# Transposing the normalised rows of a hybrid layer's first pass on TensorE through two PSUM banks, where DMA transposed them

## The chip, the cores and the metric

The kernel runs on one core of a Trainium2 chip. The metric is device time in microseconds (us) of one execution. TensorE (PE in the rows; its weight loads are PEld), VectorE (DVE), ScalarE (ACT), GpSimd (POOL) and SyncE (SP) each work off a queue of their own in order; an instruction that waits holds up all that stand behind it on its engine. In this kernel every transfer is issued from SP's queue.

## The reference

One decoder layer over 4096 rows of width 1024 (float32). What matters here is its beginning:

```
h    = rms_norm(x) * norm_gain
proj = h @ w_in            # 3328 columns: gMLP u, v, gate; attention q, k, v, gate; memory q, gate
kv   = rms_norm(mem) * mem_gain @ w_mem_kv      # 256 memory tokens
...                        # gMLP gating, dilated attention (8 heads), attention into the memory
out  = x + concat(branches) @ w_out
```

## The kernel before

Rows are worked in 32 tiles of 128. A matrix product needs its left operand transposed (the 1024 columns on partitions), and nearly full precision is had by splitting each number into a high and a low float16 part and adding three products. So `proj` issues, for each of 8 slices of 128 columns, three matmuls of 512 columns: 24 for a result of 512 columns.

The program has a first pass (pass A), two more passes over the rows (B and C, with the attention of the 8 heads interleaved) and a last loop for the output. Pass A does, for each tile n:

- `rows(n)`, three tiles ahead of the products: load x (tile name `x_a`), then `norm_rows`: ScalarE squares and sums (`xj_a`, L236), VectorE and GpSimd make the scale (`xs_a`, L237 and L238), ScalarE writes the high part and VectorE the low part of `xh_a` (L240, L241; two buffers), and the pair is transposed into `xTa` (L242; four buffers). `xTa` is also stored in device memory for passes B and C (`xTd`, L339).
- `pv`: 24 matmuls (L222) of `xTa` with the value weights, taken out of PSUM by ScalarE and VectorE into `vt` (L274, L276).
- `pq`: 24 matmuls with the query and key weights of four heads, taken out by ScalarE into `rw_q` (L248), squared (`sq_q`, L250), reduced on VectorE (L252, L258), raised to the power -1/2 on GpSimd (`r_q`, L260), scaled on VectorE (L267, L269), split into `hl` (ScalarE L287, VectorE L288), transposed by a DMA into `stgA` (L290), put in another order by GpSimd (`stpA`, L291) and stored.

`pv` and `pq` share two PSUM banks (tag `pj`). The maxima that scale the weights pass through small PSUM tiles (`pt_wV`, `pt_wQ`, `pt_wM`, L157 and L162, read last on VectorE at L179). `ps_tile` puts tag `tr` onto tag `po`, which has two banks; in pass A only these weight tiles use it. The 256 memory tokens go through `norm_rows` too (`xh_m`, into `mTs`).

The order on each engine is made by a scheduler from a model of the program when the kernel is built, so an edit of one helper can move instructions all through the program. The line that the edit replaces is the last of `norm_rows`:

```
        Q.dma_start_transpose(dst.rearrange("p a k t -> p (a k) t"),
                              hl.rearrange("p a k -> p (a k)"))
```

Of the kernel before, what the change touches and what calls it, by code (L numbers as in the profile page):

```python
# [9 lines left out]
F16 = mybir.dt.float16  # L10
# [8 lines left out]
P = 128  # L19
# [3 lines left out]
KT = D // P  # L23
# [48 lines left out]
def tile_hybrid_layer(ctx, tc, x, mem, norm_gain, w_in, gv_gain, wsT, gb, aqg, akg,  # L72
                      mem_gain, w_kv, mqg, mkg, w_out, out):
    nc = tc.nc
    V, S, G, TE, Q = nc.vector, nc.scalar, nc.gpsimd, nc.tensor, nc.sync
# [6 lines left out]
    def ps_tile(tag, shape, dt, name):  # L82
        return pp.tile(shape, dt, tag="po" if tag == "tr" else tag, name=name)
# [17 lines left out]
    idh = cp.tile([P, P], F16, name="idh")  # L101
# [124 lines left out]
    def load_rows(pool, src, nm):  # L226
        xt = pool.tile([P, D], F32, name=f"x_{nm}", tag="xin", bufs=4)
        Q.dma_start(xt, src)
        return xt

    def norm_rows(pool, src, dst, nm, xt=None):
        if xt is None:
            xt = load_rows(pool, src, nm)
        junk = pool.tile([P, D], BF16, name=f"xj_{nm}", tag="xj", bufs=1)
        ss = pool.tile([P, 2], F32, name=f"xs_{nm}", tag="xs", bufs=3)
        S.activation(junk, xt, AF.Square, accum_out=ss[:, 0:1])  # L236
        V.tensor_scalar(ss[:, 0:1], ss[:, 0:1], 2.0 ** -30, EPS * 2.0 ** -20, ALU.mult, ALU.add)  # L237
        G.tensor_tensor(ss[:, 1:2], ss[:, 0:1], mhalf[:, 0:1], ALU.pow)  # L238
        hl = pool.tile([P, 2, D], F16, name=f"xh_{nm}", tag="xh", bufs=2)
        S.activation(hl[:, 0, :], xt, AF.Copy, scale=ss[:, 1:2])  # L240
        V.scalar_tensor_tensor(hl[:, 1, :], xt, ss[:, 1:2], hl[:, 0, :], ALU.mult, ALU.subtract)  # L241
        Q.dma_start_transpose(dst.rearrange("p a k t -> p (a k) t"),  # L242
                              hl.rearrange("p a k -> p (a k)"))


    def head_rs(pool, ps, nh, scs, scales, nm):
# [81 lines left out]
    with tc.tile_pool(name="pA", bufs=2) as pA:  # L328
# [7 lines left out]
        def rows(n, xt=None):  # L336
            xTs[n] = sk.tile([P, 2, KT, P], F16, name=f"xTa{n}", tag="xT", bufs=4)
            norm_rows(pA, x[n * P:(n + 1) * P, :], xTs[n], f"a{n}", xt)
            Q.dma_start(xT_d[n], xTs[n].rearrange("p a k t -> p (a k t)"))  # L339
# [35 lines left out]
        for n in range(NT):  # L375
# [53 lines left out]
            if n == 10:  # L429
                for j in range(2):  # L430
                    norm_rows(pA, mem[j * P:(j + 1) * P, :], mTs[:, j], f"m{j}")
            if n == 12:
                wM, scM = got("wM")
                for j in range(2):
# [5 lines left out]
                    hl = pm.tile([P, 8, 2, HD], F16, name=f"mhl{j}", tag="hl", bufs=2)  # L440
# [481 lines left out]
    for n in range(NT):  # L922
        if n + 2 < NT:
            prep_y(n + 2)
        yT, a, xr = yTs.pop(n)
# [53 lines left out]
```

## Time and profile before

| | us |
|---|---|
| median of 3 runs | 2269.75 (2264.73 to 2272.71) |
| the profiled execution | 2285.33 |
| its span, first to last instruction | 2283.6 |
| from the start to the first `pq` matmul | 53.2 |
| from there to the first `pq` matmul of the 26th tile | 341.1 |
| from there to the end of pass A's products | about 73 |
| passes B and C and the output | about 1816 |

The profiled execution took 1.7 us more than its span and 15.6 us more than the median of the runs. A busy share is the time in which an engine had at least one instruction under way. "x" counts instructions. In a row on a wait, the engine and line ahead of the arrow waited, and what stands behind it ended the wait.

### The profile page before, as it was taken

The numbers are of one execution on the slowest core, as the hardware profiler recorded it, in microseconds if no ns is written. First come the engines' busy times: TensorE is split into PE (matmuls) and PEld (weight loads), VectorE is DVE, ScalarE is ACT, GpSimd is POOL, SyncE is SP. The second block draws the span as 40 slices with busy tenths as digits, with TensorE's granted clock in tenths as the row PEclk, the third lists the DMA queues.
The fourth block names the chain that finished last, engine by engine and source line by source line (L and its number), as shares of the span: only waits on it lengthen the run. The fifth ranks groups of instructions, "written<-read, shape, count | busy, mean of one in ns | idle before, by whom it ended". The sixth has DMA issues, their size and how long they took to land. (4 is left out here: it accounts for less than half of the span.)

```text
span 2283.6 us, 43678 instructions
## 1 busy us (share of the span) xinstructions
PE 2020.8 (88%) x15969; PEld 1248.7 (55%) x15969; DVE 1563.5 (68%) x4297; ACT 985.1 (43%) x1886; POOL 975.4 (43%) x696
## 2 busy tenths in 40 slices
PE   4888888978799899799999998998989998888888
PEld 3333333434356456465676775765756765555556
DVE  6776655477777778688786876876767576656553
ACT  6333432222246446465575674654757741101000
POOL 1455455465367568574464452553635520000000
PEclk8999999989899999799999998999999999999999
DMA  9999797765355765755646446345454379999996
GB/s 267 212 217 233 184 224 167 185 167 158 114 159 123 207 152 146 181 126 157 165 101 146 115 100 168 92 116 131 91 122 103 73 191 209 234 224 223 225 220 148
DMA packets 606232, 375.48 MB, mean 164 GB/s; under 512 B 431681, under 2 KB 541377, under 8 KB 604225
## 3 DMA queue, kind: packets, MB, share of 16 engines
q1 hardware_dynamic: 606016, 372.69, 67.9%
q8 instruction: 125, 2.05, 0.4%
q14 instruction: 91, 0.74, 0.1%
HBM read 198.52 MB, written 113.84 MB: 137 GB/s over the span
## 5 line engine op out<-in xcount | busy, mean ns | idle before, releaser
L521 POOL TENSOR_TENSOR pl<-e,ph 128x512 f16<-128x512 f32 (+1 forms) x384 | 414.6, 1094 | 310.0 <-ACT ph L520 231.4
L222 PE MATMUL pc<-wC,xTc 128*128 128x512 f16 (+1 forms) x2304 | 484.4, 354 | 8.7 <-DVE r_wO L160 7.6
L222 PE MATMUL fps<-wO,fyT 128*128 128x256 f16 (+1 forms) x2304 | 355.0, 317 | 48.7 <-DMA fyT<-fhl 48.6
L474 DVE CUSTOM_DVE_ANT_0 jk<-pa,mask 128x256 bf16<-128x256 f32 (+1 forms) x768 | 302.2, 393 | 62.8 <-PE pa L467 44.1
L571 ACT ACTIVATE e<-e,gas 128x512 f32<-128x512 f32 (+1 forms) x384 | 253.1, 673 | 181.2 <-DVE e L569 178.7
L222 PEld LDWEIGHTS <-fyT 128*128 128x128 f16 x2304 | 227.8, 100 | 175.0 <-DMA fyT<-fhl 55.6
L222 PEld LDWEIGHTS <-xTc 128*128 128x128 f16 x2304 | 225.5, 101 | 166.4 <-issue 25.0
L222 PEld LDWEIGHTS <-xTa 128*128 128x128 f16 x1608 | 164.9, 103 | 265.3 <-issue 95.9
L569 DVE TENSOR_TENSOR e<-s,mask 128x512 f32<-128x512 f32 (+1 forms) x384 | 234.0, 625 | 75.9 <-PE s L566 57.5
L222 PEld LDWEIGHTS <-xTb 128*128 128x128 f16 x1536 | 152.7, 101 | 179.2 <-issue 31.5
L222 PE MATMUL pv<-wV,xTa 128*128 128x512 f16 (+1 forms) x840 | 195.5, 396 | 52.8 <-DVE vt L276 37.0
L520 ACT CAST ph<-e 128x512 f16<-128x512 f32 (+1 forms) x384 | 211.5, 567 | 31.0 <-PE o L591 19.6
L222 PE MATMUL pqb<-wQ,xTb 128*128 128x512 f16 x768 | 196.9, 400 | 11.5 <-DMA xTb<-xTd 7.4
L291 POOL COPY stpA<-stgA 128x1024 f16<-128x1024 f16 x32 | 153.0, 4801 | 103.3 <-DMA stgA<-hl 52.3
L564 PE MATMUL s<-q,k 128*128 128x256 f16 (+1 forms) x768 | 180.9, 267 | 16.2 <-DMA q<-qkpd 7.9
L291 POOL COPY stpB<-stgB 128x1024 f16<-128x1024 f16 x32 | 153.6, 4800 | 96.4 <-DMA stgB<-hl 75.6
L222 PE MATMUL pag<-wAG,xTb 128*128 128x512 f16 x768 | 188.2, 389 | 3.9 <-DVE sg L699 3.6
L222 PE MATMUL pq<-wQ,xTa 128*128 128x512 f16 x768 | 175.7, 386 | 16.0 <-ACT rw_q L248 11.0
L467 PE MATMUL pa<-kp,qn 128*128 128x256 f16 (+1 forms) x768 | 139.3, 271 | 48.8 <-DVE mx L474 41.3
L741 ACT ACTIVATE fhl<-fy,fa 128x1024 f16<-128x1024 f32 x32 | 36.7, 1148 | 333.2 <-DMA fyT<-fhl 328.2
L566 PE MATMUL s<-q,k 65*128 65x256 f16 (+1 forms) x768 | 173.1, 268 | 3.1 <-DMA q<-cm 3.1
L587 PE MATMUL o<-vr,ph 128*128 128x65 f16 x1368 | 169.9, 194 | 3.5 <-ACT ot L596 2.4
(271 smaller groups left out, 3502.7 us busy)
## 6 DMA issues: line engine op xcount, KB each, us to landing
vr<-vd SPq DMA_DIRECT2D x48, 520.0 KB
fo<-od SPq DMA_DIRECT2D x96, 260.0 KB
od<-ot SPq DMA_DIRECT2D x128, 130.0 KB
x_a<-in_x_dram SPq DMA_DIRECT2D x32, 512.0 KB
xTd<-xTa SPq DMA_DIRECT2D x32, 512.0 KB
xTb<-xTd SPq DMA_DIRECT2D x32, 512.0 KB
xTc<-xTd SPq DMA_DIRECT2D x32, 512.0 KB
fx<-in_x_dram SPq DMA_DIRECT2D x32, 512.0 KB
```

Source lines behind the costliest of these rows:

```text
L222: TE.matmul(ps[:, :n], xt[:, a, k, :], w[:, b, k, c:c + n], start=(k == 0 and a == 0 and b == 0), stop=(k == KT - 1 and a == 1))
L291: G.tensor_copy(stp[:, :, half].rearrange("p s (r j) -> p s j r", r=R16), stg[:, :, half].rearrange("p s (j r) -> p s j r", r=R16))
L467: TE.matmul(pa[:, i, 256 - w:256], qn[:, q0:q0 + (P - 1) * d + 1:d], packed(kp, d, r, max(b - 1, 0), w), start=True, stop=True)
L474: V.tensor_tensor_reduce(jk[:, :w], pa[:, i, 256 - w:256], masks[d][:, 256 - w:256], 1.0, -3e38, ALU.add, ALU.max, mx[:, mc:mc + 1])
L520: S.copy(ph[:, :w], e[:, :w])
L521: G.tensor_sub(pl[:, :w], e[:, :w], ph[:, :w])
L564: TE.matmul(st[:, i, :n], k1[:, kk], packed(q1, d, r, b, n), start=True, stop=False)
L566: TE.matmul(st[:, i, :n], k2[:, kk], packed(q2, d, r, b, n), start=False, stop=True)
L569: V.tensor_tensor(e[:, :w], st.rearrange("p a q -> p (a q)")[:, :w], masks[d][:, :w], ALU.add)
L571: S.activation(e[:, :w], e[:, :w], AF.Exp, scale=asg[:, 2:3])
L587: TE.matmul(o[:, slot, 0:65], hi[:, c:c + 128], v[:, 0:65], start=(j == 0), stop=False)
L741: S.activation(hl[:, 0, :], y, AF.Copy, scale=a[:, 1:2])
```

## The change

`norm_rows` calls a new function `transposed`. TensorE transposes the 8 slices of the high part into one PSUM bank and the 8 slices of the low part into the other (tag `po`, float16, multiplied by a float16 identity), ScalarE copies the first bank into `xTa`, and VectorE the second. It holds for the 32 tiles of x and the two tiles of memory tokens. The other DMA transposes (of `hl`, and those of later passes) stay.

```diff
         S.activation(hl[:, 0, :], xt, AF.Copy, scale=ss[:, 1:2])
         V.scalar_tensor_tensor(hl[:, 1, :], xt, ss[:, 1:2], hl[:, 0, :], ALU.mult, ALU.subtract)
-        Q.dma_start_transpose(dst.rearrange("p a k t -> p (a k) t"),
-                              hl.rearrange("p a k -> p (a k)"))
+        transposed(dst, hl, nm)
+
+    def transposed(dst, hl, nm):
+        for a in range(2):
+            pt = ps_tile("po", [P, KT, P], F16, f"pt{nm}_{a}")
+            for k in range(KT):
+                TE.transpose(pt[:, k, :], hl[:, a, k * P:(k + 1) * P], idh)
+            if a == 0:
+                S.copy(dst[:, a], pt)
+            else:
+                V.tensor_copy(dst[:, a], pt)
```

Lines behind the edit stand 9 further down in the changed kernel (L248 becomes L257). Three places show what the scheduler made of it; numbers at the ends of names tell tiles apart.

ScalarE in the middle of pass A, one tile's worth of rows, before:

```order
L240 ACTIVATE xh_a_2412<-x_a_2405,xs_a_2408 128x1024
L274 ACTIVATE vt_2218<-pv_2193 128x8x64
L236 ACTIVATE xj_a_2707,xs_a_2708<-x_a_2705 128x1024
L287 CAST hl_15_2169<-rw_q_15_2155 128x8x64
L248 COPY rw_q_16_2250<-pq_2223 128x512
L250 ACTIVATE sq_q_16_2252<-rw_q_16_2250 128x512
```

and after:

```order
L257 COPY rw_q_14_2448<-pq_2421 128x512
L250 COPY xTa_2467<-pta_0_2478 128x1024
L259 ACTIVATE sq_q_14_2450<-rw_q_14_2448 128x512
L240 ACTIVATE xh_a_2701<-x_a_2694,xs_a_2697 128x1024
L236 ACTIVATE xj_a_3093,xs_a_3094<-x_a_3091 128x1024
L283 ACTIVATE vt_2524<-pv_2499 128x8x64
L296 CAST hl_14_2462<-rw_q_14_2448 128x8x64
```

The copy out of the first bank (`pta_0`) has come between the two instructions that take up a `pq`, and `xh_a` now follows it.

GpSimd in the middle of pass A, before:

```order
L260 TENSOR_TENSOR r_q_17_2347<-r_q_17_2347,mhalf 128x8
L291 COPY stpA_2249<-stgA_2248 128x8x8x16
L275 MEMSET vt_2563 128x8x2
L238 TENSOR_TENSOR xs_a_2887<-xs_a_2887,mhalf 128x1
L291 COPY stpA_2249<-stgA_2248 128x8x8x16
L260 TENSOR_TENSOR r_q_18_2478<-r_q_18_2478,mhalf 128x8
L275 MEMSET vt_2653 128x8x2
```

and after:

```order
L300 COPY stpA_2140<-stgA_2139 128x8x8x16
L269 TENSOR_TENSOR r_q_14_2452<-r_q_14_2452,mhalf 128x8
L238 TENSOR_TENSOR xs_a_3094<-xs_a_3094,mhalf 128x1
L284 MEMSET vt_2636 128x8x2
L300 COPY stpA_2447<-stgA_2446 128x8x8x16
L269 TENSOR_TENSOR r_q_15_2558<-r_q_15_2558,mhalf 128x8
L238 TENSOR_TENSOR xs_a_3202<-xs_a_3202,mhalf 128x1
```

Before, the power of one tile (`r_q_17`) stands ahead of the reordering copies of the two tiles before it; after, the copy of the tile before always stands ahead of a tile's power.

TensorE where a weight tile's maximum is broadcast (L162) in the middle of pass A, before:

```order
L222 LDWEIGHTS xTa_1729
L222 MATMUL pq_2130<-wQ_204,xTa_1729 128x512
L162 MATMUL pt_wQ_2493<-r_wQ_2495,ones_185 128x2
L222 LDWEIGHTS xTa_1908
L222 MATMUL pv_2193<-wV,xTa_1908 128x512
```

and after:

```order
L162 MATMUL pt_wQ_2803<-r_wQ_2805,ones_185 128x2
L222 LDWEIGHTS xTa_2467
L222 MATMUL pv_2873<-wV,xTa_2467 128x512
L248 LDWEIGHTS xh_a_2849
L248 MATMUL pta_1_2862<-idh,xh_a_2849 128x128
```

One product behind the broadcast there now stands a transpose, whose bank is the one that `pt_wQ` holds. Four weight tiles in the middle of pass A (two of `wM`, two of `wQ`) stand so.

## Rows read from the trace of the kernel before

**Rows 1.** The page: the span, and TensorE's busy time (share of the span).

```profile
span 2283.6 us, 43678 instructions
...
PE 2020.8 (88%) x15969; PEld 1248.7 (55%) x15969; DVE 1563.5 (68%) x4297; ACT 985.1 (43%) x1886; POOL 975.4 (43%) x696
```

**Rows 2.** Stretches: window, length, engines' busy us, granted clock, DMA share, GB/s.

```profile
0.00:53.00 53.00, 24.35 (x156) 18.31 (x157) 37.49 (x111) 30.77 (x64) 8.50 (x31) 0.91 0.96 265
53.00:394.00 341.00, 287.12 (x1218) 124.60 (x1218) 216.31 (x385) 132.29 (x232) 169.77 (x98) 0.92 0.93 206
394.00:467.00 73.00, 68.90 (x312) 30.62 (x310) 35.69 (x57) 19.93 (x35) 40.07 (x19) 0.98 0.74 179
467.00:2283.00 1816.00, 1640.40 (x14286) 1075.13 (x14284) 1274.05 (x3745) 802.14 (x1556) 757.06 (x550) 0.95 0.63 153
```

**Rows 3.** Waits from 53 to 394 us: us in total, times, longest.

```profile
ACT xh_a L240 <- DMA xTa<-xh_a: 79.4, 19, 8.8
...
POOL stpA L291 <- DMA stgA<-hl: 37.7, 13, 7.1
...
PE pv L222 <- DVE vt L276: 33.9, 13, 4.0
...
PE pq L222 <- ACT rw_q L248: 10.1, 4, 3.9
```

**Rows 4.** Instructions on `xTa`: ns shortest/median/longest, first and last start in us.

```profile
L222 PE MATMUL pq<-wQ,xTa x768: 376/379/634, 53.2 to 467.4; 128*128 128x512 f16 x192
L242 SPq DMA_TRANSPOSE xTa<-xh_a x32: 1806/3949/7421, 10.4 to 428.9; - x32
```

**Rows 5.** Timeline of TensorE: start, length of a run of instructions, what.

```profile
332.97 5.34 PE L222 MATMUL pv<-wV,xTa 128*128 128x512 f16 x24 [0.65 <-DVE vt L276]
...
638.48 0.45 PE L491 MATMUL pm<-idh,mv 128*32 128x128 f16 x5
```

**Rows 6.** Single lines: ns shortest/median/longest, first and last start in us.

```profile
L491 PE MATMUL pm<-idh,mv x40: 219/219/230, 638.5 to 1692.0; 128*8 128x128 f16 x32, 128*32 128x128 f16 x8
...
L596 ACT COPY ot<-o x192: 348/370/462, 666.7 to 1840.4; 128x260 f32<-128x260 f32 x192
...
L276 DVE SCALAR_TENSOR_TENSOR vt<-pv,vt x31: 401/680/693, 49.9 to 463.4; 128x512 f16<-128x512 f32 x29, 128x256 f16<-128x256 f32 x2
...
L241 DVE SCALAR_TENSOR_TENSOR xh_a<-x_a,xs_a,xh_a x32: 1272/1286/5057, 9.1 to 413.7; 128x1024 f16<-128x1024 f32 x32
```

**Rows 7.** Timeline, 436 to 450 us: one tile's way through GpSimd.

```profile
436.57 1.64 POOL L260 TENSOR_TENSOR r_q<-r_q,mhalf 128x8 f32<-128x8 f32 x1
...
439.95 0.58 ACT L248 COPY rw_q<-pq 128x512 f32<-128x512 f32 x1
440.08 0.69 DVE L288 TENSOR_TENSOR hl<-rw_q,hl 128x512 f16<-128x512 f32 x1 [0.68 <-ACT hl L287]
...
440.80 1.24 SPq L290 DMA_TRANSPOSE stgA<-hl  x1
...
443.58 4.74 POOL L291 COPY stpA<-stgA 128x1024 f16<-128x1024 f16 x1 [5.31 <-DMA stgA<-hl]
...
447.93 1.65 POOL L260 TENSOR_TENSOR r_q<-r_q,mhalf 128x8 f32<-128x8 f32 x1
```

**Rows 8.** Timeline, 0 to 75 us: the start of pass A.

```profile
17.22 6.47 PE L222 MATMUL pv<-wV,xTa 128*128 128x256 f16 x31 [4.82 <-DMA xTa<-xh_a]
...
21.71 10.28 SPq L242 DMA_TRANSPOSE xTa<-xh_a  x2
...
26.25 0.38 PE L162 MATMUL pt_wV<-r_wV,ones 1*128 1x2 f32 x2 [0.59 <-DVE r_wV L161]
...
28.13 0.15 DVE L179 TENSOR_SCALAR sc_wV<-pt_wV 128x1 f32<-128x1 f32 x1
...
31.65 6.81 PE L222 MATMUL pv<-wV,xTa 128*128 128x256 f16 x38 [5.03 <-DMA xTa<-xh_a]
```

**Rows 9.** Timeline of TensorE: the first `pq` of the first and of the 26th tile.

```profile
53.22 1.01 PE L222 MATMUL pq<-wQ,xTa 128*128 128x512 f16 x2 [1.75 <-ACT wQ L172]
...
394.27 1.03 PE L222 MATMUL pq<-wQ,xTa 128*128 128x512 f16 x4
```

## The prediction

> **What bounds the kernel now.** I read the page, then the stretches of pass A, the waits in its middle, the instructions on `xTa`, and last two pieces of timeline. The page says that TensorE is busy for 88% of a span of 2283.6 us [rows 1]: on the whole this is a TensorE kernel, and what the change is worth must be found in the stretches in which it acts. Those are pass A's: its start (0 to 53 us), its middle (53 to 394) and its last tiles (394 to 467) [rows 2]. There the DMA share is 0.96, 0.93 and 0.74, against 0.63 later.
>
> How far is the middle from TensorE's own limit? 24 matmuls of 512 columns that follow each other closely took 5.34 us [rows 5]; the last of them lasts 0.379 [rows 4], so they start (5.34 - 0.379) / 23 = 0.2157 us apart, and the 48 of a tile take 10.35. The middle holds 1218 records [rows 2]: 1218 x 0.2157 = 262.7 us of 341. About 54 us are idle (341 - 287.1 busy), and 24 us of the busy time went to half clock: the mean granted clock is 0.92, so (1 - 0.92) / 0.5 = 16% of 341 = 55 us stood at 1.2 GHz, which costs half of that, 27, much the same.
>
> What TensorE idled for is PSUM: 33.9 us on `vt` and 10.1 on `rw_q`, evictions by VectorE and ScalarE [rows 3]. ScalarE was busy for only 132 of 341 us, so it was late because it stood: it waited 79.4 us, 19 times, up to 8.8 each, in `xh_a` (L240) for the DMA transposes `xTa<-xh_a` that still read the buffer which it wanted to overwrite [rows 3]. Queued behind `xh_a` on ScalarE are just `vt`, `hl` and `rw_q`, as its order shows. So the transposes hold ScalarE, ScalarE holds PSUM, and PSUM holds TensorE.
>
> **What goes.** 34 DMA transposes. Each occupies SP's queue for 3.95 us at the median [rows 4], 134 us in all, with the x and weight loads behind it. Each moves 128 x 2048 x 2 bytes = 0.52 MB, 17.8 MB in all; at the middle's 206 GB/s with a share of 0.93, 221 GB/s when full, that is 81 us of the DMA engines. The 79.4 us of waiting on ScalarE go with them, because TensorE will have read `xh_a` long before.
>
> **What comes, on TensorE.** 34 x 16 = 544 transposes of 128 columns. The kernel has such an operation: five of them took 0.45 us [rows 5], one lasts 219 ns [rows 6], so they start (0.45 - 0.219) / 4 = 0.058 us apart. The bounds are 0.058 and 0.219; I take 0.058, for 16 stand in a row. A tile then costs 0.92 us more, all 34 cost 31.5, and a tile's floor is 11.3. The Trainium skill's page "TensorE: Matmul & The Clock Gate", Part 4: PE-mode transpose, puts one at some 275 ns in a kernel's context; by that, with none overlapping, the 544 would take 150 us and the sum below would be +94 in place of -24.5. The row agrees with such a length (219) and not with such a distance.
>
> **On ScalarE and VectorE.** ScalarE copies 1024 float16 out of PSUM: 0.58 us for 512 elements [rows 7] and 0.37 for 260 [rows 6] make 0.82 ns an element, so 1.0 us. It has the room: 132 + 27 x 1.0 = 159 us busy in the middle. For VectorE the nearest is `vt`, 512 elements from PSUM in 0.68 [rows 6]: 1.2 for 1024 (bounds 0.6, if 16-bit elements go in pairs, and 5.1, the longest `xh_a` [rows 6], if such a copy is held as that one was). `vt` never passed 0.693 in 31 times though it too reads PSUM, hence the low value. VectorE would be busy for 216 + 32 = 248 us.
>
> **The new pace of the middle.** With ScalarE free, the next loop is through GpSimd. The order after has a tile's `stpA` ahead of the next tile's `r_q`, always. Then power, scaling, `hl`, DMA transpose, `stpA`, next power make a ring. In rows 7 it ran so once, nearly undisturbed: from 436.57 to 447.93 us, 11.4, with 2.8 from the issue of the transpose to `stpA`. So at best the ring is as quick as TensorE's 11.3. `stpA` waited for its transpose 2.9 us on average where it waited, up to 7.1 [rows 3]; part of that goes with the large transposes. I take 11.9 a tile (bounds 11.4 and 13.2, today's pace: 341.05 us from the first tile to the 26th [rows 9], less 10.35 for the memory tokens' 48 matmuls, over 25 tiles).
>
> New middle: TensorE's work 262.7 + 27 tiles x 0.92 = 287.5; the ring, 0.6 x 26 = 16; four places where a transpose waits for the bank of a weight tile, from the broadcast to its last reader 28.13 + 0.15 - 26.25 = 2.0 us each [rows 8], 8 (bounds 0 and 16; what is queued behind it on TensorE is a product, so it counts in full); and half clock, a third of today's 27 since it followed the idling, 9. Together 320.5, that is 20.5 less (bounds: 296, -45, and 341, 0).
>
> **The start.** TensorE waited 4.82 + 5.03 us for `xTa` [rows 8], and two transposes held SP for 10.28 with a weight load behind them. Against that stand some five copies on VectorE (busy for 37 of 53 us): 6 us. I take -6 (bounds -12 and 0).
>
> **The last tiles and the rest.** From 394 on TensorE is near its floor; two more tiles' transposes cost 1.8: +2. The last three tiles have no rows left to transpose. Passes B and C and the output are the same instructions; the scheduler has moved them among each other, by some tens of places in the middle of the program, and I put this at 0 with 8 us either way, 0.4% of 1816, which is a judgement.
>
> Sum: -20.5 - 6 + 2 = -24.5. The profiled execution took 2285.33, 1.7 more than its span, so a profile of the changed kernel should take about 2261; on the scale of the runs, 2269.75 - 24.5 = **2245 us**.
>
> **Rivals.** (a) The ring through GpSimd takes the place of the wait: `stpA` late by 2 us in each tile leaves the pace at 13.2. The middle stays at 341, the start gives 6, the last six tiles, now at 11.7, lose 1.5 each: 9 - 6 = +3, about 2273. For it: the strict order, and `stpA`'s 37.7 us of waiting. Against: that waiting came with a DMA share of 0.93, and the ring at 432 to 450 us kept to 11.4.
>
> (b) All goes at TensorE's floor: middle 296, start -12, some 55 in all: 2214. For it: evictions were all that TensorE waited for. Against: the ring has no slack.
>
> (c) Slower, through TensorE's clock. Today 16% of the middle is at 1.2 GHz. If the transposes between the products let the clock fall more often, it costs what the waits give back: a TensorE that is slower also covers the ring's 16 us, so the gain is gone when the loss at half clock reaches 9 + 24.5 + 16 = 50 us, which is 100 us of the middle at 1.2 GHz, a mean grant of 0.85. At 0.80 it loses 68, and the time is 2269.75 + 18 = 2288. For it: a stretch with much idling does fall. Against: today's five transposes at 638 stand amid products, and without idling the last tiles got 0.98. The Trainium skill says, on the same page and in the same part, that transposes don't count as busy for the clock gate. No row here settles this.
>
> (d) Transposes that do not overlap: 544 x (0.219 - 0.058) = 88 us more on TensorE, about 2333. The row of five speaks plainly against it.
>
> **How the numbers follow.** My forecast (-10 to -45): 0.63. (b): 0.09. (a): 0.13. (c): 0.10. (d): 0.02. Passes B and C off by more than the 8 allowed, either way: 0.03. The likeliest case gives the time; 8 in 10 are held by 2218 (towards b) to 2274 (takes in a, leaves c and d out). The likeliest case alone runs from 2225 to 2260. About 0.3%, 7 us, is what a measurement of this kernel can tell from no change. Faster by more: 0.63 + 0.09 = 0.72 with the larger share of the last 0.03 set against edges of (a); within: 0.13; slower by more: 0.10 + 0.02 and the rest, 0.15.
>
> **What would show it.** In the changed kernel's profile: no wait of `xh_a` on a DMA; transposes (L248) about 58 ns apart; copies near 1.0 and 1.2 us; the first `pq` near 47 us and the 26th near 368; a DMA share of about 0.75 in the middle; and `stpA` followed at once by `r_q`. I am wrong if pass A still ends near 467 us, if the middle's granted clock is below 0.85, or if the stretch behind pass A changes length by more than 8 us.

## The result and the profile after

The changed kernel took 2291.81 us (median of 4 runs, 2285.06 to 2296.01) against 2267.24 for the kernel before in the same sitting (4 runs, 2261.01 to 2272.71): a ratio of 1.0093, 95% interval 1.0071 to 1.0116. I had forecast a gain of 24.5 us; it lost 21 to 25. The profiled execution of after took 2292.64 us, like its other runs; that of before, 2285.33, was longer than any of its timed runs, so lengths in the two profiles are compared with some 10 us of doubt for the whole program, less for a stretch.

The stretches of the changed kernel, in the columns of [rows 2]:

```profile
0.00:53.00 53.00, 29.62 (x211) 23.51 (x211) 37.93 (x113) 32.59 (x64) 8.32 (x31) 0.88 0.69 219
53.00:394.00 341.00, 306.88 (x1706) 151.81 (x1706) 215.93 (x405) 157.22 (x262) 172.03 (x98) 0.95 0.65 170
394.00:467.00 73.00, 63.80 (x311) 29.26 (x309) 25.55 (x68) 19.00 (x35) 34.53 (x20) 0.98 0.56 138
467.00:2283.00 1816.00, 1634.48 (x14269) 1074.58 (x14268) 1271.36 (x3745) 803.51 (x1559) 756.77 (x549) 0.96 0.64 153
```

What the change was to do, it did. The DMA share of the middle fell from 0.93 to 0.65, TensorE's busy time rose by 20 us, ScalarE's by 25, and the clock did not fall: 0.95 against 0.92 [rows 2]. The new operations, by line:

```profile
L248 PE MATMUL pta<-idh,xh_a x512: 218/219/314, 7.4 to 423.3; 128*128 128x128 f16 x171
...
L250 ACT COPY xTa<-pta x32: 989/1015/1019, 8.7 to 428.0; 128x1024 f16<-128x1024 f16 x32
...
L252 DVE COPY xTa<-pta x32: 677/684/692, 11.8 to 428.3; 128x1024 f16<-128x1024 f16 x32
```

The waits from 53 to 394 us, in the columns of [rows 3]:

```profile
ACT hl L296 <- DVE rw_q L278: 103.5, 21, 11.7
POOL stpA L300 <- DMA stgA<-hl: 83.1, 17, 11.8
DVE rw_q L276 <- POOL r_q L269: 60.1, 20, 10.7
...
PE pv L222 <- ACT rw_q L257: 14.6, 2, 11.5
...
PE pv L222 <- DVE vt L285: 13.0, 6, 4.5
```

The row with 79.4 us at the head of [rows 3], ScalarE's `xh_a` behind a DMA, is gone. In its place stands the ring: `stpA`'s wait for its DMA transpose went from 37.7 to 83.1 us, and `hl` and `rw_q`, which follow the power, wait 103.5 and 60.1. The first and the 26th tile's `pq` on TensorE's timeline, as in [rows 9]:

```profile
56.23 1.01 PE L222 MATMUL pq<-wQ,xTa 128*128 128x512 f16 x2 [0.42 <-ACT wQ L172]
...
386.27 1.46 PE L222 MATMUL pq<-wQ,xTa 128*128 128x512 f16 x6
```

The start is 3 us later, the middle 11 shorter (330.0 against 341.1), and from the 26th tile to the end of the last `pq` it takes 82.2 us where it took 73.5. So pass A ends at 468.5 us, before it was 467.8: nothing is left of what the missing DMA transposes gave. Of the 24.6 us between the medians some 20 or more are then lost behind it. The two profiles alone don't show that loss: in them the stretch behind pass A is 6.6 us longer (1822.4 against 1815.8), because the profiled execution of before was 15.6 us above its median.

The turn with the copy's longest wait for its transpose, around tile 16:

```profile
281.60 1.66 POOL L269 TENSOR_TENSOR r_q<-r_q,mhalf 128x8 f32<-128x8 f32 x1
...
283.11 0.43 SPq L306 DMA_DIRECT2D qkpd<-stpA  x1
283.59 1.06 SPq L351 DMA_DIRECT2D vd<-vt  x1
...
285.13 0.69 DVE L297 TENSOR_TENSOR hl<-rw_q,hl 128x512 f16<-128x512 f32 x1 [0.68 <-ACT hl L296]
...
291.21 0.33 SPq L323 DMA_DIRECT2D kp<-qkpd  x1
291.64 1.27 SPq L299 DMA_TRANSPOSE stgA<-hl  x1
...
295.67 4.71 POOL L300 COPY stpA<-stgA 128x1024 f16<-128x1024 f16 x1 [11.84 <-DMA stgA<-hl]
299.99 1.65 POOL L269 TENSOR_TENSOR r_q<-r_q,mhalf 128x8 f32<-128x8 f32 x1
```

The halves are ready at 285.8, but SP's queue stands behind `kp<-qkpd`, a load of head 0 that has to wait for a write issued at 283.1; the transpose goes out at 291.6, the copy starts at 295.7, and the next power at 300.0: 18.4 us for one turn. Some turns are longer for other reasons: 25.2 us from the power at 323.62, when VectorE was held up by a weight tile's preparation, and 21.2 from 223.9, with the memory tokens in between.

The copy does not always stand ahead of the next tile's power, as I had read from the order. In 9 of 31 turns the power ran first, 6 of them in the middle, and the copy then started right behind it, beside VectorE's scaling:

```profile
149.47 1.64 POOL L269 TENSOR_TENSOR r_q<-r_q,mhalf 128x8 f32<-128x8 f32 x1 [4.83 <-DVE m_wM L149]
...
151.82 4.75 POOL L300 COPY stpA<-stgA 128x1024 f16<-128x1024 f16 x1 [0.65 <-DMA stgA<-hl]
151.88 4.34 DVE L278 TENSOR_TENSOR rw_q<-rw_q,gaq 128x256 f32<-128x256 f32 x1
```

The scaling by `gaq` (L278) took 4.34 us here, and 0.42 without a copy beside it. The experiments come back to this.

### The profile page after: what moved, and what is told of

The parts are those of the page before. It is cut to its first block, busy times and chain, and to the rows that moved or that the text cites. A ratio compares the mean times of both kernels' runs of the same rounds, so it can differ in the third digit from the quotient of the medians.

```text
span 2290.9 us, 44788 instructions
## 1 busy us (share of the span) xinstructions
PE 2037.2 (89%) x16513; PEld 1281.0 (56%) x16513; DVE 1551.5 (68%) x4331; ACT 1012.3 (44%) x1920; POOL 971.7 (42%) x696
## 4 chain that ended last, share of the span: by engine, by line
PE 41%; DMA 14%; DVE 7%; ACT 3%; issue 3%; POOL 2%; SPq 1%; DVEq 0%; POOLq 0%; ACTq 0%
PE pc L222 12%; PE fps L222 11%; DMA fyT<-fhl 7%; PE pqb L222 3%; PE s L573 2%; PE s L575 2%; PE pag L222 2%; DMA qm<-q2t 2%; PE pa L476 2%; DVE e L578 1%; DMA cm<-rw 1%; POOL pl L530 1%; PE o L600 1%; PE o L598 1%; PE o L596 1%
## 5 line engine op out<-in xcount | busy, mean ns | idle before, releaser
L222 PE MATMUL pv<-wV,xTa 128*128 128x512 f16 (+1 forms) x840 | 183.7, 376 | 28.2 <-ACT rw_q L257 14.6
L573 PE MATMUL s<-q,k 128*128 128x256 f16 (+1 forms) x768 | 176.2, 264 | 18.2 <-DVE e L578 10.0
L598 PE MATMUL o<-vr,ph 128*128 128x64 f16 x1368 | 170.4, 194 | 0.0
```

What stands on the lines that cost most here:

```text
L222: TE.matmul(ps[:, :n], xt[:, a, k, :], w[:, b, k, c:c + n], start=(k == 0 and a == 0 and b == 0), stop=(k == KT - 1 and a == 1))
L573: TE.matmul(st[:, i, :n], k1[:, kk], packed(q1, d, r, b, n), start=True, stop=False)
L598: TE.matmul(o[:, slot, 0:64], hi[:, c:c + 128], v[:, 66:130], start=False, stop=False)
```

## The experiments

Three questions: does the ring set pass A's pace, what lost the time behind pass A, and does a saving in pass A reach the end. "Pass A alone" means that all behind pass A is left out and zeros are written. The five groups (e1 to e4, e5 to e8, and so on; e17 and e18) ran on five chips, on which the kernel before took from 2262.5 to 2286.0 us, 1% apart. Ratios of full programs are to the kernel before on the same chip. Times of pass A alone are safe within a group; e7, e8, e13 and e17 are set beside e1 across chips, which can account for some 4 us with e7 and e8 and 2 with e13 and e17. In the tables "middle" is from the first to the 26th tile's `pq`, "end" the end of the last.

**e1, e2: pass A alone, with the change and without.** The edit, in both:

```
-    at_cm = tc.tile_pool(name="at", bufs=2)
...
+    tc.strict_bb_all_engine_barrier()
+    for n in range(NT):
+        Q.dma_start(out[n * P:(n + 1) * P, :], zr)
```

> The changed kernel cut off behind pass A: passes B and C, the attention and the output loop are left out, and zeros are written to the output instead (32 writes of 512 KB behind a barrier, the same in all four kernels of this group). Theory 1 (the change gains a little in pass A, and the whole program loses it behind): the first 26 tiles came 8 us earlier in the full trace (386.3 against 394.3), so this one ends 5 to 15 us before its counterpart without the change. Rival 2 (pass A itself is no faster or is slower with the change): within 3 us of the counterpart, or behind it.

> The kernel before, cut off behind pass A in the same way (the same parts left out, zeros written). It is the counterpart of the run above: theory 1 has it 5 to 15 us longer than the changed one, rival 2 level with it or shorter.

548.17 us (544.77 to 549.7) and 552.49 (549.89 to 553.88): 4.3 us shorter with the change. Middle 337.4 and 345.5, end 472.2 and 480.1. A little was gained, between the 5 that theory 1 asked for and the 3 of rival 2; the +21 of the whole program is not in pass A.

**e3, e4: the copy `stgA` into `stpA` on ScalarE.** With the change and without, pass A alone:

```
-        G.tensor_copy(stp...
+        (S.copy if g == 0 else G.tensor_copy)(stp...
```

> The changed kernel's pass A alone (same parts left out, zeros written), with the copy stgA into stpA on ScalarE instead of GpSimd, so that the power of the next tile no longer stands behind 4.8 us of copy on GpSimd. Theory 1 (the ring power, scaling, halves, DMA transpose, copy, next power sets the pace of about 12 us a tile): the pace falls to 10.6 to 11, and the program is 20 to 35 us shorter than the changed pass A alone. Rival 2 (TensorE with its transposes and the banks of the weight preparation set the pace): within 5 us of it. Rival 3 (ScalarE now waits for the DMA transpose in its turn, and the ring closes there): longer by more than 5 us.

> The kernel before, pass A alone, with the same move of the copy to ScalarE. If the transposes of x by DMA set the pace there (13.2 us a tile), the move changes nothing: within 5 us of the counterpart without it, and the change is then worth 25 to 45 us between this run and the changed one with the move. If the ring through GpSimd sets the pace before too, it is 15 us shorter or more.

615.6 and 602.64 us: 67 and 50 longer. For e3 rival 3 held; neither expectation for e4 had it longer. The copy takes as long on ScalarE as on GpSimd, and ScalarE, which also empties PSUM, now stands for the DMA transpose in its own queue (e3):

```profile
L300 ACT COPY stpA<-stgA x32: 4713/4747/5033, 83.1 to 557.8; 128x1024 f16<-128x1024 f16 x32
...
ACT stpA L300 <- DMA stgA<-hl: 70.7, 21, 8.0
```

**e5, e6: the order behind pass A held.** The work behind pass A is the same 20,509 instructions in both programs, but the scheduler's simulated clock arrives there at another time and orders them otherwise. e5 is the changed kernel with them chained, on each engine, in the order of the kernel before; e6 the kernel before with the order of the changed one:

```
+    for i0, i1 in zip(seq, seq[1:]):
+        tc.add_manual_dep(i1, i0.name, mybir.DependencyInfo(
+            mybir.DependencyClass.NoSync, mybir.DependencyReason.DATA), reason="order")
```

> The changed kernel in full, with every instruction behind pass A (passes B and C, attention, output loop) held on its engine in the order that the scheduler gave it in the kernel before. Pass A alone was 4.3 us shorter with the change (548.17 against 552.49 us). Theory 1 (the loss behind pass A is nothing but the other order that the scheduler gave that work): 2 to 8 us shorter than the kernel before, a ratio of 0.9965 to 0.999. Rival 2 (the transposes by TensorE leave something behind that slows the rest, whatever its order): as slow as the changed kernel was, 1.007 to 1.012.

> The kernel before in full, its pass A untouched (transposes by DMA), with every instruction behind pass A held in the order that the scheduler gave it in the changed kernel. Theory 1 (the order costs the time): 20 to 32 us slower than the kernel before, a ratio of 1.009 to 1.014, without any transpose by TensorE. Rival 2 (something that the transposes leave behind): level with the kernel before, 0.998 to 1.002.

e5: 2267.12 us, ratio 1.0022 (1.0004 to 1.004), 5 us slower. e6: 2276.19, ratio 1.005 (1.0027 to 1.0072), 11 us slower without one transpose by TensorE. Theory 1 had the direction of both and was too bold in size: the order costs 11 us by e6, 16 by the step from the change to e5, and about 5 us of the change's loss are not the order. That holding an order costs nothing in itself is not shown: no run holds the kernel before in its own order and changes nothing else (e16 below, with its own order held and one further edit, stands at 0.9999). Pass A ended at 470.6 and 471.4, that is level.

**e7, e8: breaking the ring in two places.** Pass A alone. e7 queues a tile's copy on GpSimd, with the write that follows it (`flush`), behind the next tile's power; with that, e7 also issues each of head 0's loads one tile later, since they read what is written there. e8 leaves these loads out.

```
         qn = qk_split(pool, ps, 8, scs, f"q{g}_{n}", agn, 4)
+        if late:
+            with tc.issue_after(pows[-1].ins):
+                flush()
...
-            if n % 8 == 7:
-                load_max(0, (n - 7) * P, (n + 1) * P)
+            if n == NT - 1:
+                flush()
+            if n and n % 8 == 0 or n == NT - 1:
+                load_max(0, (n - 1) // 8 * 8 * P, ((n - 1) // 8 + 1) * 8 * P)
```

```
-            if n % 8 == 7:
-                load_max(0, (n - 7) * P, (n + 1) * P)
```

> The changed kernel's pass A alone (the rest left out, zeros written, as in e1), with the copy stgA into stpA of a tile queued on GpSimd behind the power of the next tile, so that no power waits for a DMA transpose through GpSimd's queue. Theory 1 (the ring through GpSimd sets the pace): the 26 middle tiles, 337 us in e1, fall to 295 to 315, and the program from 548 to 510 to 530 us. Rival 2 (TensorE, the weight preparation or ScalarE's order set it, and the ring only looks long because others wait): 543 to 550 us.

> The changed kernel's pass A alone (as in e1), without the loads of the first head's keys and queries that pass A issues on the sync engine's queue behind every eighth tile (they are left out). In the full trace the halves' DMA transpose of tile 16 was issued about 6 us after its halves, behind such a load that waited. Theory 1 (the ring stands still when its transpose is held in that queue): four loads' stalls go, 6 to 14 us shorter than 548. Rival 2 (the queue is not what holds the transposes): within 3 us.

529.07 and 530.85 us, against 548.17 in e1. e8 gained 17.3 us, some 13 of them if 4 are the chip's, where theory 1 gave it 6 to 14; 5 were in the last tiles and 8 in the middle. e7's total just fits, the reason given for it does not: its middle stayed at 336.7 us (295 to 315 expected) and only the last tiles were quicker, 10.8 us a tile against 12.5, which it may owe to the later loads (e8, without them, took 11.6). So GpSimd's queue was not all of it. VectorE by line in the middle; mean ns stand behind the busy time. From e1:

```profile
L276 DVE TENSOR_TENSOR rw_q<-rw_q,r_q 128x512 f32<-128x512 f32 x24 | 24.2, 1008 | 59.4 <-POOL r_q L269 59.3
```

From e7, where the line is L278, and then the copy and this operation on the timeline:

```profile
L278 DVE TENSOR_TENSOR rw_q<-rw_q,r_q 128x512 f32<-128x512 f32 x25 | 63.7, 2549 | 30.3 <-POOL r_q L271 30.2
...
L263 DVE TENSOR_REDUCE r_q<-sq_q 128x8 f32<-128x512 f32 x25 | 17.1, 683 | 12.8 <-ACT sq_q L261 12.7
...
L287 DVE SCALAR_TENSOR_TENSOR vt<-pv,vt 128x512 f16<-128x512 f32 x22 | 15.0, 682 | 1.4 <-ACT vt L285 1.4
```

```profile
366.96 4.76 POOL L314 COPY stpA<-stgA 128x1024 f16<-128x1024 f16 x1
367.04 4.58 DVE L278 TENSOR_TENSOR rw_q<-rw_q,r_q 128x512 f32<-128x512 f32 x1 [1.42 <-POOL r_q L271]
```

The product of `rw_q` with `r_q`, 0.69 us alone, ends within 0.1 us of the copy that began just before it. In e7 the copy stands right behind the power, where VectorE wants to scale: in 16 of the 32 tiles the scaling began during the copy and took 4.57 us at the median, in the other 16 never more than 0.69. So what GpSimd's queue no longer held, VectorE now waited out. The reduction, with one input, and `vt`, with one in PSUM, keep their lengths. The Trainium skill, "SBUF — State Buffer", section "Who interferes with whom", says it so: a VectorE instruction with two SBUF inputs and a GpSimd instruction that reads SBUF exclude each other, the later one waiting for the whole of the earlier. The rows agree, at 4.58 us against 0.69.

**e9 to e12: e7's edit in full programs.** e9 is the changed kernel with it and its own order behind; e10 with the order of before; e11 is e10 with head 0's loads issued two tiles later; e12 is the kernel before with the edit, and its own order held. All four have the loads one tile later, as e7. e11's further edit:

```
+            if n % 8 == 2 and n > 2:
+                with tc.issue_after(turn[-1].ins):
+                    load_max(0, (n - 10) * P, (n - 2) * P)
```

> The changed kernel in full, with the copy of pass A on GpSimd queued behind the next tile's power (as in e7), and the order behind pass A left to the scheduler. Pass A alone went from 548.2 to 529.1 us by it. Theory 1 (ring in pass A, and a drawn order behind it): 19 us less than the changed kernel's +21 to +25, with the order another draw of some 15 us either way: a ratio of 0.994 to 1.008. Rival 2 (what pass A gains is given back behind it, since the attention's side work or the DMA queues have no room earlier): 1.007 or more.

> The same kernel, with everything behind pass A held in the order of the kernel before (as in e5, which stood at 1.0022). Theory 1: 4.5 - 19 = 14 us shorter than the kernel before, a ratio of 0.991 to 0.997, the first version that beats it. Rival 2 (given back behind): 0.999 to 1.004, as e5.

> As e10, and the first head's loads in pass A are issued two tiles later, behind a DMA transpose of halves, so that the sync engine's queue does not stand on a write that has not landed (leaving those loads out was worth 17 us in e8, with the ring closed). Theory 1 (both stop the same ring, so their gains overlap): 0 to 8 us below e10. Rival 2 (the queue holds other transposes and writes too): 10 us or more below e10. Rival 3 (the ring is no longer what waits): level with e10.

> The kernel before (transposes by DMA), with the copy queued behind the next power, and its own order behind pass A. Theory 1 (before the change the DMA transposes of x set the pace, and the ring only where they let it): 0 to 8 us shorter than before, 0.9965 to 1.000, so that the change is worth 8 us or more once the ring is cut. Rival 2 (the ring was as much of the wait before the change): 12 us shorter or more, level with e10; then the transposes by TensorE bring nothing.

| run | us | ratio, 95% interval | middle | end of pass A |
|---|---|---|---|---|
| e9 | 2290.75 | 1.0107, 1.0076 to 1.0137 | 336.3 | 461.2 |
| e10 | 2267.24 | 1.0016, 0.9995 to 1.0037 | 336.5 | 462.2 |
| e11 | 2266.99 | 1.0015, 0.9995 to 1.0035 | 338.2 | 463.1 |
| e12 | 2279.73 | 1.0062, 1.0039 to 1.0085 | 337.9 | 464.8 |

A miss for theory 1: e9 and e10 lie where rival 2 (given back behind) had them, e11 is level with e10, its rival 3, and e12, slower than before, is outside both of its expectations. Pass A ends 8.4 us sooner in e10 than in e5 (462.2 against 470.6), not 19; in e7 too the last `pq` had ended only 11.8 us sooner than in e1 (460.4 against 472.2), and the rest of the 19 lay behind it. Of the 8.4 nothing reached the end. e9 and e10 differ by 23.5 us in the order behind pass A alone. Where e10 loses its lead shows in part: VectorE's operations stand 15 us ahead of e5's at 640 us and 3 at 1060, and from 750 to 900 us the granted clock is 0.94 where e5 has 0.99, which is (0.05 / 0.5) x 150 = 15 us more at 1.2 GHz and costs up to 7.5. The rest, and e12's 14 us, stay open.

**e13 to e16: the copy on VectorE.** The edit of e3 with `V.tensor_copy`: e13 the change and e14 before, pass A alone; e15 and e16 the same in full, order of before.

> The changed kernel's pass A alone (the rest left out, zeros written, as in e1: 548.2 us), with the copy stgA into stpA on VectorE instead of GpSimd. Theory 1, now changed (the copy on GpSimd keeps VectorE's operations with two SBUF inputs out for up to 4.7 us each time): those operations are back at their lengths alone (0.69, 0.42, 1.28 us), and the middle 26 tiles fall from 337 to 295 to 315 us, the program to 505 to 525. Rival 2 (the copy's stride of 16 elements makes it 4.7 us on VectorE too, as it did on ScalarE): 550 us or more. Rival 3 (TensorE's clock and the weight preparation set the middle): 540 to 550 us.

> The kernel before, pass A alone (552.5 us as in e2), with the copy on VectorE. Theory 1: the scaling of x (L241), 1.28 us alone and 2.3 us beside the copy, comes back to 1.28, and the DMA transposes of x then set the pace alone: 525 to 548 us, and the change is worth 15 to 35 us once the copy is away from GpSimd. If the DMA transposes cost nothing themselves: level with e13.

> The changed kernel in full, the copy of pass A on VectorE, everything behind pass A held in the order of the kernel before (e5 without the move: 1.0022). Theory 1, if what pass A saves reaches the end: 20 to 35 us below e5, a ratio of 0.987 to 0.994. If it is given back in pass B as in e10: 0.998 to 1.003. Rival 2 (the copy slow on VectorE): 1.004 or more.

> The kernel before in full, with the copy of pass A on VectorE and its own order behind pass A. Theory 1, if it reaches the end: 5 to 25 us below the kernel before, 0.989 to 0.998, and e15 lies 10 us or more below this one. If given back: 0.999 to 1.004.

| run | us | ratio of full programs | middle | end of pass A |
|---|---|---|---|---|
| e13 | 559.4 | | 351.6 | 488.5 |
| e14 | 541.42 | | 337.6 | 469.3 |
| e15 | 2304.67 | 1.0084, 1.0058 to 1.0109 | 358.4 | 497.4 |
| e16 | 2286.6 | 0.9999, 0.9978 to 1.0019 | 339.5 | 474.5 |

With the change it is worse again: e13 has the time of its rival 2, but not for the reason given there, since the copy took 2.46 us and not 4.7; e15 the same. Without the change e14 is 11 us shorter than e2, as theory 1 had it, and in full, in e16, this is given back. The lengths came back in e13, as theory 1 said (`rw_q` by `r_q` 692 ns), and the copy takes half as long, but VectorE has to take it in its order and stands for the DMA transpose. From e13:

```profile
L300 DVE COPY stpA<-stgA 128x1024 f16<-128x1024 f16 x23 | 56.5, 2457 | 70.9 <-DMA stgA<-hl 70.9
L241 DVE SCALAR_TENSOR_TENSOR xh_a<-x_a,xs_a,xh_a 128x1024 f16<-128x1024 f32 x24 | 30.9, 1289 | 1.1 <-ACT iv_wQ L166 0.6 <-ACT xh_a L240 0.5
```

The two costs of the copy, keeping VectorE out and making its own engine wait, had been traded for each other in e7 and here.

**e17, e18: against both.** The copy on VectorE, and queued there behind the low halves of the next tile, when its transpose has long landed, and head 0's loads one tile later, as in e7; e17 pass A alone, e18 in full with the order of before:

```
+        sub = V.tensor_sub(hl[:, :, 1, :], qn, hl[:, :, 0, :])
...
+            with tc.issue_after(sub.ins):
+                flush()
...
+            (V if g == 0 else G).tensor_copy(stp...
```

> The changed kernel's pass A alone (the rest left out, zeros written, as in e1: 548.2 us), with the copy on VectorE and queued there behind the low halves of the next tile, so that its DMA transpose has landed long before. Theory 1 (the copy's place alone holds the pace): no waits of VectorE for a DMA transpose, no lengthened operations, 26 middle tiles in 300 to 320 us instead of 337, the program at 510 to 528. Rival 2 (VectorE, now with 2.45 us more a tile, or the weight preparation's work on it is the bound): 530 to 548.

> The same in the full program, with everything behind pass A in the order of the kernel before (e5: 1.0022, e10: 1.0016). If what pass A saves reaches the end: a ratio of 0.989 to 0.995. If pass B gives it back, as it did the 8 us of e10: 0.998 to 1.002.

e17: 488.18 us, 60 less than e1, and a middle of 296.4, both better than theory 1 had them. It has the loads of e7, so against e7 only the copy's engine and place differ, and that took the middle from 336.7 to 296.4; the weight tiles' preparation and TensorE's products, which are the same, were thus not what held it. How much of the 60 the later loads give (leaving them out was worth up to 17 in e8) is not separated. e18: 2234.93 us (2230.29 to 2238.52, 5 runs) against 2270.55 (9 runs), a ratio of 0.9841 (0.9814 to 0.9868): it beats both kernels, by more than its expectation of 0.989 to 0.995, and most of what pass A saves reaches the end. Stretches and waits of e18's middle:

```profile
53.00:394.00 341.00, 330.55 (x1863) 163.71 (x1862) 251.10 (x465) 169.05 (x279) 79.51 (x82) 0.98 0.74 189
394.00:467.00 73.00, 65.97 (x295) 30.08 (x294) 54.97 (x143) 23.11 (x48) 22.97 (x11) 0.93 0.74 180
```

```profile
POOL r_q L273 <- DVE r_q L271: 142.3, 24, 9.6
...
ACT rw_q L261 <- PE pq L224: 50.7, 19, 4.1
...
DVE rw_q L280 <- POOL r_q L273: 29.2, 21, 1.6
```

No DMA transpose stands among the waits that the view lists any more; GpSimd waits for VectorE, ScalarE for TensorE, and TensorE is busy for 330.6 of 341 us at a clock of 0.98. The middle takes 300.8 us, the last tiles 70.7, and pass A ends at 425.5, 45 us before e5's; the program is about 41 shorter than e5's by the two ratios, (1.0022 - 0.9841) x 2270.

What e18 owes to the transposes and what to the moved copy is not separated: the kernel before with this copy was not run. When the copy was on VectorE (e14), its ScalarE still waited for the DMA transposes of x, for 104.5 us in the middle:

```profile
ACT xh_a L240 <- DMA xTa<-xh_a: 104.5, 22, 9.2
```

That speaks for the transposes, but e14's copy was not moved behind the halves. What the change is worth depends on where the copy stands: in pass A alone it gains 4.3 us with the copy on GpSimd (e1, e2) and loses 13 with it on ScalarE (e3, e4) and 18 on VectorE (e13, e14); in full, with the copy behind the next power, it is some 10 us better (1.0016 in e10, 1.0062 in e12).

## Why the prediction was wrong

**The steps that failed** are two: the pace of the ring, "I take 11.9 a tile", and the rest of the program, put at 0. Against the sum of -24.5 stand +21 to +25, some 46 to 49 us more: 9.5 in the middle, 6.7 in the last tiles, 9 at the start, and some 20 or more behind pass A, the largest term.

The ring first. Measured: (330.0 - 10.35) / 25 = 12.8 in the middle, and 12.8 again over the last six tiles, where before the change it was 11.4. In the terms of my sum:

```profile
56.23:386.27 330.04, 296.62 (x1640) 145.61 (x1640) 210.50 (x396) 152.25 (x255) 168.28 (x97) 0.96 0.65 170
```

TensorE was busy for 296.6 us, where the work of 287.5 and the 9 for half clock make 296.5 (so close by luck: a grant of 0.96 would cost 13); it stood idle for 33.4, where I had 16 for the ring and 8 for the banks of weight tiles. Most of the 33.4 are waits for `rw_q` (14.6) and `vt` (13.0) out of PSUM, listed above; the four places of a bank hardly show. I had named the ring, and rival (a) said that it would take the wait's place, though with a middle of 341, 11 us too long; but I took its length from one turn "nearly undisturbed" and gave each tile half a microsecond for the rest. Two things that lie in no row of that turn lengthen it. The wait for the transpose grows with SP's queue (11.84 us at tile 16), and leaving head 0's loads out was worth some 13 to 17 us in e8. And GpSimd's copy does not only stand in its own queue: VectorE's scaling, with two SBUF inputs, waits it out when the copy comes behind the power, as at 151.88 us above; e7 had this in half of all tiles, and in e17 it is gone. How the 0.9 us a tile divide between these two is not separated. The row was there to be read: `xh_a` on VectorE up to 5057 ns at a median of 1286 [rows 6]. I used it as a far bound for another copy and did not ask what held it.

The price: the middle was 9.5 us longer than forecast (330.0 against 320.5), and the last tiles +8.7 where I had +2, at a pace of 12.8 us a tile there too, above TensorE's 11.3.

**The start**, -6 forecast, +3 measured. The waits for `xTa` are gone, but TensorE's next wait there is 6.73 us at 33.47, for the weight scale `r_wV`, which stands behind the load of a gain and a scaling of x in VectorE's order:

```profile
27.48 0.23 DVE L120 TENSOR_TENSOR gmq<-cst 128x64 f32<-128x64 f32 x1 [4.12 <-DMA cst<-in_mem_k_gain_dram]
...
32.01 1.28 DVE L241 SCALAR_TENSOR_TENSOR xh_a<-x_a,xs_a,xh_a 128x1024 f16<-128x1024 f32 x1 [1.51 <-ACT xh_a L240]
...
33.47 0.58 PE L162 MATMUL pt_wV<-r_wV,ones 1*128 1x2 f32 x2 [6.73 <-DVE gms L127]
```

A wait that is removed counts only as far as the next one lies behind it.

**The rest**, 0 with 8 us either way, "which is a judgement": the order alone costs 11 us (e6) to 16 (the change against e5), and the same pass A with one order or the other differs by 23.5 (e9, e10). This is half or more of the loss; what makes one order slower than the other stays open.

**What was right.** That the transposes overlap, and their spacing, 0.058 us forecast and (0.61 - 0.219) / 7 = 0.056 measured in this row:

```profile
287.00 0.61 PE L248 MATMUL pta<-idh,xh_a 128*128 128x128 f16 x8
```

With the copy out of the way the middle, products and transposes together, took 296.4 us in e17, where I had 287.5 as TensorE's floor and 296 as the lower bound; rival (d) fell. The 275 ns of the Trainium skill ("TensorE: Matmul & The Clock Gate", Part 4: PE-mode transpose) is near the length of one, 219 here, and not the distance of two. ScalarE's copy, 1.0 forecast, 1.015. VectorE's copy came out shorter, 1.2 forecast, 0.684, near the bound of 0.6. The clock did not fall: rival (c), at 0.85 or less, against 0.95. The DMA share, 0.75 forecast, is 0.65. Of my own signs for "wrong", one came true to the letter: pass A still ends near 467 us. The third, more than 8 us behind pass A, came true by the timed runs (some 20) and not by the two profiles (6.6).

## What to carry to other kernels

When a wait is removed, go round the ring that comes next with the durations it has beside its neighbours, not with those of its best turn; a median far below the longest says that something holds the operation, and it should be named before the forecast is made. An operation that waits for a DMA is worth trying behind the work of the next tile on its engine. Here that was shown on VectorE alone: in full programs, the copy moved to another place in GpSimd's queue (e10) or to VectorE (e15) gained nothing or lost, and with both, and the loads a tile later as in e10, the program was some 41 us shorter than e5. And where a scheduler orders the program by a simulated clock, a local edit draws a new order for all that follows: hold the old order to see what the edit itself does.

## What the runs showed of the hardware

- A copy of 1024 float16 per partition with a stride of 16 elements took 4.7 us on GpSimd, 4.75 on ScalarE and 2.45 on VectorE, while a copy of 1024 float16 in order out of PSUM took 1.015 on ScalarE and 0.684 on VectorE.
- GpSimd's strided copy stretched VectorE's operations with two SBUF inputs that began beside it to its own end: 0.69 to 4.58 us (e7), 0.42 to 4.34 (after); also the scaling of x without the change, 1.28 us alone, 2.32 on average in e2's middle. Operations with one input in PSUM kept 0.68.
- Transposes of 128 columns, each 219 ns long, started 0.056 us apart in a row of eight (after). Sixteen a tile amid products left the granted clock at 0.98 in e18.
